# Gate weights' low parts by adding DMAs onto negated high parts, and an earlier place for a norm's parameters

## The chip, the core and the metric

The kernel runs on one core of a Trainium2 chip. A core has TensorE (PE, the matrix engine, with a weight-load queue PEld), VectorE (DVE), ScalarE (ACT), GpSimd (POOL) and SyncE (SP), each with a queue of instructions of its own that it works off in order, and 16 DMA engines that move data between the chip's main memory and the core's on-chip memory SBUF. Matmul results land in the banks of PSUM. The metric is the device time of one execution in microseconds.

## The reference

A decoder trunk of two layers over 256 rows of width 1024, all in float32. Each layer has four sub-layers, each followed by a norm over the residual sum:

```
x = LN(a*x + 0.5 * (silu(x Wgate) * (x Wup)) Wout)       first feed-forward
x = LN(a*x + mixer(x))                                     forgetting attention in layer 0, latent attention in layer 1
x = LN(a*x + 0.5 * (silu(x Wgate) * (x Wup)) Wout)       second feed-forward
x = LN(a*x + sigmoid(x Wg + bg) * (p[i] Wp))              gated sub-layer
```

LN subtracts the mean, divides by the deviation, multiplies by a gain vector g and adds a vector b. Layer 1's attention reads keys and values made from x at the end of layer 0 ("kv" below).

## The kernel before, in words

**Two parts for each operand.** A float32 matrix product is made of three products of rounded operands: the high part of a weight is the weight rounded to the matrix engine's format, its low part is the weight minus the high part; the same is done for x. The three products are high x high, high x low and low x high. So every weight is loaded raw from main memory, ACT copies it into a high part (line 246) and DVE subtracts that from the raw weight for the low part (line 247). A unit is half a load: 128x1024 elements of high and as many of low, in one slot (ten slots hl0 to hl9, and others on loan, named gb, qk, fs, ota, otb). Raw loads are groups of 1 MB or less in three buffers (raw), all issued by SP (lines 457 to 491); a buffer is free for the next group when both units of its last group have been split.

**Who orders the work.** The kernel runs its program once as a recorder, which yields the order in which units are used, and then for real. A planner (class Stream) follows estimated clocks of PE, ACT and DVE; after each triple of products it may put the next unit's split at that place of the ACT and DVE queues (`pump`, line 378), when the load should have come and ACT and DVE are not more than 1.6 us ahead of PE. A unit that is not split when it is needed is split there and then (`use`, line 390).

**The gated sub-layer** (`ple`, line 1052). The gate's weights Wg are eight units, key "pg", for both halves of the rows. The product x Wg is done for the first 128 rows (eight units, each three products into each of two banks), then for the last 128 rows with the same units. Before the last two units of the first half the transposes of the second half of x stand (`XT(1)`, line 1085); ACT and DVE make the two parts of the transposed x (xT, lines 623 and 627). After each half ACT takes the sigmoid (line 1075), DVE multiplies by the projected p (line 1076), adds to x and gathers statistics (lines 683, 684), POOL raises the variance to the power -1/2 (line 694), and DVE applies the norm in four instructions (line 702): two that subtract the mean and multiply by g, two that multiply by the root and add b, taken in turn for the two halves of the columns. g and b stand in one tile, gb, loaded by SP (line 668).

**What stands around it in layer 0.** Ahead of it the second feed-forward ends with its norm for each half of the rows, by the same lines 683 to 702. Behind it the queues go on with the weights of the shared keys (key "kd", 128x640 a unit) and those of layer 1's first feed-forward ("win", from in_ffn_in), whose products for the first rows come before the transposes of the last rows. In layer 1 the sub-layer is the end of the program: the second half of the rows goes by quarters of the columns, and SP stores x.

POOL in the kernel before issues no DMA; all of them are SP's.

Of the kernel before, what the change touches and what calls it, by code (L numbers as in the profile page):

```python
# [12 lines left out]
AF = mybir.ActivationFunctionType  # L13
ALU = mybir.AluOpType
# [14 lines left out]
SLACK_NS = 1600.0  # L29
# [100 lines left out]
class Recorder:  # L130
    def __init__(self):
        self.seq = []

    def use(self, key):
        self.seq.append(key)
        return Dummy()

    def pump(self, *a, **k):
        pass
# [5 lines left out]
class Stream:  # L145
# [74 lines left out]
    def split(self, half=False):  # L220
# [45 lines left out]
        self.pair(n)  # L266
        self.split_done(key, w)

    def aside(self, key):
        return self.side and key[0] == "ws" and key[-1] == 3  # L270

# [106 lines left out]
    def pump(self):  # L378

        if self.ready == len(self.order) or not self.free() or self.hold or self.order[self.ready] == self.stop:  # L380
            return
        arrival = self.arrives.get(group_of(self.order[self.ready]), 1e12)
        if arrival <= self.pe_t + 500 and max(self.act_t, self.dve_t) <= self.pe_t + SLACK_NS:
            key = self.order[self.ready]
            if self.sums_left(key):
                self.add(group_of(key))
            else:
                self.split()
# [19 lines left out]
def group_of(key):  # L408
    k = key[0]
    if k in ("win", "wiu", "fv", "kd", "dq"):  # L410
        return key[:-1] + (key[-1] // 2,)
    if k == "ws":
        return key[:-1]
    if k in ("wout", "fvb", "fvc", "fk", "fq", "fo", "pg", "pp", "mo", "qr"):
        return key[:-1] + (key[-1] // 2,)
    if k in ("kvk", "qn"):
        return ("kq", key[-1])
    return key
# [38 lines left out]
def make_loads(a):  # L457
    def loads(q, g, raw, fine, between):
        k, i = g[0], g[-1]
        if k in ("win", "wiu"):  # L460
            w = a[g[2]][0][g[1], g[3], i]
            if fine == 1:
                for k0 in range(4):
                    between.pop((i, k0), lambda: None)()
                    for h in range(2 if (i, k0) == (0, 0) else 1):
                        c = slice(512 * k0 + 256 * h, 512 * (k0 + 1) if i or k0 else 256 * (h + 1))
                        q.dma_start(raw[:, c], a["w00"][h] if (i, k0) == (0, 0) else a["w0"][4 * i + k0 - 1])
                return
            for k0 in range(0, 4, fine):
                c = slice(512 * k0, 512 * (k0 + fine))  # L470
                q.dma_start(raw[:, c], w[:, c])
        elif k in ("wout", "ws"):
            q.dma_start(raw, a[g[2]][1][g[1], i])
        elif k in ("fv", "fo", "mo", "fk", "fq"):
            q.dma_start(raw, a[k][i])
        elif k == "fvb":
            q.dma_start(raw, a[k])
        elif k in ("fvc", "qr"):
            w = a[f"{k}{i}"]
            q.dma_start(raw[:, 0 : w.shape[1]], w)  # L480
        elif k in ("pg", "pp"):
            q.dma_start(raw, a[k][g[1], i])
        elif k == "pb":
            q.dma_start(raw[0:1, 0:1024], a["ple_b_gate"][g[1] : g[1] + 1, :])
        elif k in ("kd", "dq", "kvv", "kq"):
            w = a[k][i]
            q.dma_start(raw[:, 0 : w.shape[1]], w)
        else:
            raise KeyError(g)

    return loads
# [13 lines left out]
class Trunk:  # L505
    def __init__(self, nc, pools, a, S, rec, fox_c=None):
        self.nc, self.a, self.S, self.fox_c = nc, a, S, fox_c
        self.sb, self.ps = pools
# [9 lines left out]
    def own(self, shape, dt, tag):  # L518

        self.S.check(tag)  # L520
        return self.tl(shape, dt, tag, 1)
# [8 lines left out]
    def home(self, homes):  # L530

        if self.rec:
            return None, Dummy()
        self.S.retire()
        tag = next(t for t in homes if t not in self.S.slot_of.values() and t not in self.taken)
        self.taken.add(tag)
# [6 lines left out]
    def use(self, key):  # L543
        w = self.S.use(key)
        if self.bg:
# [506 lines left out]
    def ple(self, li, last):  # L1052
        nc, S = self.nc, self.S
        y, st = {}, {}

        def bias(t, blocks):
            w = self.use(("pb", li))
            for c0, c1 in blocks:
                y[t, c0] = self.bank("y")
                self.mm(y[t, c0][:, 0 : c1 - c0], self.ones, w[:, 0, c0:c1], True, False)  # L1060

        def gate(t, k, blocks):
            w = self.use(("pg", li, k))
            for c0, c1 in blocks:
                self.mm3(
                    y[t, c0][:, 0 : c1 - c0], lambda i: self.xT[:, t, i, k, :],
                    lambda i: w[:, i, c0:c1], False, k == 7,
                )

        def post(t, c0, c1):  # L1070
            if t not in st:
                st[t] = [self.tl([128, 4, 6], F32, "st4", 2), self.tl([128, D], F32, "g4", 6), 0]
            s, sg, j = st[t]
            g = sg[:, c0:c1]
            nc.scalar.activation(g, y[t, c0][:, 0 : c1 - c0], AF.Sigmoid)
            nc.vector.tensor_tensor(g, g, self.pj[:, 2 * t + c0 // 512, c0 % 512 : c0 % 512 + c1 - c0], op=ALU.mult)  # L1076
            self.ln_stats(s[:, j, :], t, c0, c1 - c0, g, ALPHA)
            self.S.busy(act=c1 - c0, dve=c1 - c0)
            st[t][2] = j + 1

        full = ((0, 512), (512, 1024))
        bias(0, full)
        for k in range(8):
            if k == 6:
                self.XT(1)
            gate(0, k, full)
        for c0, c1 in full:
            post(0, c0, c1)
        self.ln_apply(0, st[0][0][:, 0:2, :], LN_EPS)
        quarters = tuple((c, c + 256) for c in range(0, 1024, 256))  # L1090
        if not last:
            bias(1, full)
            for k in range(8):
                if k == 6:
                    self.XT(0)
                gate(1, k, full)
            for c0, c1 in full:
                post(1, c0, c1)
            self.ln_apply(1, st[1][0][:, 0:2, :], LN_EPS)
            S.lend("ota")  # L1100
        else:
            self.store(0)
            for c0, c1 in quarters:
                bias(1, ((c0, c1),))
                for k in range(8):
                    gate(1, k, ((c0, c1),))
                post(1, c0, c1)
            self.ln_apply(1, st[1][0], LN_EPS, True)
            self.store(1, ENDS)
# [706 lines left out]
    def run(self):  # L1816
        S = self.S
        ple = lambda li: {6: [lambda: self.ple_load(li)]}
        self.ffn(0, "ffn1", 0, at={3: [self.load_x]}, cold=True, after=("ota", "otb", "qk"))
        self.fox(0)  # L1820
        self.ffn(0, "ffn2", 2, ple=True, at=ple(0), after=("otb", "qk", "fs"))
        self.load_gb(0, 3)
        self.kv_setup()
        self.ple(0, False)
        S.reclaim("fs")
        self.ffn(1, "ffn1", 0, kv=True, after=("otb", "qk"))
        self.mla(1)
        self.ffn(1, "ffn2", 2, ple=True, at=ple(1), after=("otb", "qk", "fs"))
        self.load_gb(1, 3)
        self.ple(1, True)  # L1830


@with_exitstack
def tile_trunk(ctx: ExitStack, tc: tile.TileContext, a):
    nc = tc.nc
    sb = ctx.enter_context(tc.tile_pool(name="sb", bufs=1))
    raw = ctx.enter_context(tc.tile_pool(name="raw", bufs=NRAW))
    ps = ctx.enter_context(tc.tile_pool(name="ps", bufs=1, space=bass.MemoryType.PSUM))
    dr = ctx.enter_context(tc.tile_pool(name="dr", bufs=1, space=bass.MemoryType.DRAM))
    ctx.enter_context(tc.manual_schedule())  # L1840
    a = dict(a)
    for n in ("ffn1", "ffn2"):
        a[n] = (a[n + "_in"], a[n + "_out"])
    r = Recorder()
    d = Dummy()
    Trunk(d, (d, d), d, r, True).run()
    S = Stream(nc, raw, sb, make_loads(a), r.seq)
    Trunk(nc, (sb, ps), a, S, False, dr.tile([16, 256], F32, name="fox_c")).run()


# [79 lines left out]
```

## Time and profile before

| | |
|---|---|
| median of 3 runs | 1053.96 us (1053.19 to 1055.26) |
| profiled execution | 1054.48 us |
| its span, first to last instruction | 1052.7 us |
| granted TensorE clock | 0.998 |
| gated sub-layer, layer 0 | PE from 484.6 to 510.2 us of the span |
| gated sub-layer, layer 1 | PE from 1019.9 to 1044.1 us |

Times in the profile are microseconds from the start of the span. In a timeline a row has the start, the duration, engine, line, operation, what it writes from what, shape and count; in brackets how long the engine stood idle before it and what ended that. A merged row with a count above one lasts from its first start to its last end. Instructions of DVE and ACT overlap a little: two copies of 1.04 us follow each other in 0.94. Matmul durations overlap too.

### The profile page before, as it was taken

What the parts mean: (1) busy time and instruction counts of PE and PEld (TensorE: products, weight loads), DVE (VectorE), ACT (ScalarE), POOL (GpSimd) and SP (SyncE); (2) the same over time, 40 slices, a digit from 0 to 9 for tenths busy, and PEclk for the clock granted to TensorE, in tenths of its full rate; (3) what the DMA queues carried; (4) which work ended last, traced back from release to release, by engine and by line L of the source; (5) the groups of instructions that cost most, each with busy time, mean ns of one, the idle gap of its engine ahead of it and who ended that gap; (6) DMA issues with size and microseconds to landing.
All of it is one profiled execution on the core that took longest, in us unless ns stands there. A gap on an engine that the chain in (4) does not pass through costs nothing.

```text
span 1052.7 us, 17554 instructions
## 1 busy us (share of the span) xinstructions
PE 1037.3 (99%) x7085; PEld 949.7 (90%) x7085; DVE 895.0 (85%) x1312; ACT 592.5 (56%) x901; POOL 59.9 (6%) x88
## 2 busy tenths in 40 slices
PE   9999999999999999999899999999999999999996
PEld 8999898999889999998799898988899889898986
DVE  5788976868898979978979899898887989899877
ACT  6565563667745554663465646546776564646541
POOL 0000000123300000000220000000000000000000
PEclk9999999999999999999999999999999999999999
DMA  7855586444736374673564555742444564554732
GB/s 280 307 186 188 194 287 242 161 144 159 257 126 240 120 249 144 219 301 140 190 234 157 201 195 168 277 154 105 151 155 170 184 213 156 184 213 174 279 121 81
DMA packets 37477, 202.74 MB, mean 193 GB/s; under 512 B 3970, under 2 KB 9874, under 8 KB 16532
## 3 DMA queue, kind: packets, MB, share of 16 engines
q1 hardware_dynamic: 37396, 201.63, 54.0%
q8 instruction: 55, 0.90, 0.3%
q14 instruction: 26, 0.21, 0.1%
HBM read 200.55 MB, written 1.06 MB: 192 GB/s over the span
## 4 chain that ended last, share of the span: by engine, by line
PE 68%; DVE 3%; ACT 1%; issue 1%; POOL 0%; DVEq 0%; ACTq 0%; POOLq 0%
PE h L610 37%; PE y L610 21%; PE tr L610 8%; PE tr L614 2%; DVE hl L247 1%; DVE x L702 0%; PE h L614 0%; DVE x L683 0%; DVE st L684 0%; DVE g L1076 0%; ACT hl L246 0%; POOL rs L694 0%; DVE tr L1715 0%; ACT qk L623 0%; ACT P L1340 0%
## 5 line engine op out<-in xcount | busy, mean ns | idle before, releaser
L610 PE MATMUL h<-xT,hl 128*128 128x256 f32 x3144 | 366.9, 278 | 0.2 <-DVE hl L323 0.2
L610 PEld LDWEIGHTS h<-xT,hl 128*128 128x128 f32 x3144 | 362.8, 189 | 2.0 <-ACT xT L623 0.6
L247 DVE TENSOR_TENSOR hl<-raw,hl 128x1024 fp32r<-128x1024 f32 (+4 forms) x273 | 317.3, 1191 | 38.8 <-ACT hl L246 37.6
L246 ACT ACTIVATE hl<-raw 128x1024 fp32r<-128x1024 f32 (+4 forms) x273 | 270.0, 1027 | 72.0 <-DVE raw L302 41.0
L610 PE MATMUL y<-hl,g 128*128 128x512 f32 x336 | 78.6, 391 | 0.0
L610 PEld LDWEIGHTS y<-hl,g 128*128 128x128 f32 x336 | 62.6, 188 | 12.6
L610 PE MATMUL h<-hl,xT 128*128 128x512 f32 (+2 forms) x312 | 68.0, 371 | 0.0
L610 PEld LDWEIGHTS h<-hl,xT 128*128 128x128 f32 x312 | 54.9, 188 | 9.8
L610 PE MATMUL y<-hl,otb 128*128 128x512 f32 x219 | 58.0, 399 | 0.0
L610 PE MATMUL y<-hl,xT 128*128 128x512 f32 (+3 forms) x282 | 52.7, 334 | 0.0
L623 ACT ACTIVATE xT<-tr 128x512 fp32r<-128x512 f32 x28 | 16.3, 597 | 61.7 <-PE tr L614 61.6
L258 DVE TENSOR_TENSOR hl<-raw,hl 128x1024 fp32r<-128x1024 f32 (+2 forms) x42 | 49.7, 1188 | 1.3 <-ACT hl L254 1.2
L254 ACT ACTIVATE hl<-raw 128x1024 fp32r<-128x1024 f32 (+2 forms) x42 | 43.0, 1028 | 9.7 <-DVE raw L302 9.2
L610 PEld LDWEIGHTS y<-hl,xT 128*128 128x128 f32 x282 | 44.1, 188 | 4.6 <-ACT xT L623 0.4
L610 PEld LDWEIGHTS y<-hl,otb 128*128 128x128 f32 x219 | 39.8, 188 | 8.3 <-DVE otb L627 0.3
L610 PE MATMUL y<-hl,ota 128*128 128x512 f32 x177 | 46.7, 398 | 0.1
L694 POOL TENSOR_TENSOR rs<-ve,mhalf 128x1 f32<-128x1 f32 x16 | 15.1, 944 | 522.2 <-DVE ve L693 522.2
L610 PE MATMUL tr<-xT,hl 128*128 128x256 f32 x360 | 42.8, 278 | 0.0
L610 PEld LDWEIGHTS tr<-xT,hl 128*128 128x128 f32 x360 | 42.1, 188 | 0.3
L610 PEld LDWEIGHTS y<-hl,ota 128*128 128x128 f32 x177 | 32.8, 189 | 7.7 <-DVE hl L247 0.6
L820 ACT ACTIVATE P<-h 128x512 f32<-128x512 f32 x33 | 19.7, 596 | 33.2 <-PE h L610 32.8
L294 DVE TENSOR_TENSOR ts<-raw 128x1024 f32<-128x1024 f32 x29 | 35.4, 1222 | 0.6
(324 smaller groups left out, 1638.5 us busy)
## 6 DMA issues: line engine op xcount, KB each, us to landing
raw<-in_ffn_in_dram SPq DMA_DIRECT2D x85, 1024.0 KB, 4.9
raw<-in_ffn_out_dram SPq DMA_DIRECT2D x44, 1024.0 KB, 5.0
raw<-in_pg_dram SPq DMA_DIRECT2D x8, 1024.0 KB, 4.8
raw<-in_mo_dram SPq DMA_DIRECT2D x8, 1024.0 KB, 4.8
raw<-in_kq_dram SPq DMA_DIRECT2D x8, 640.0 KB, 4.2
gb<-in_ln_g_dram SPq DMA_DIRECT2D x8, 512.0 KB, 6.2
gb<-in_ln_b_dram SPq DMA_DIRECT2D x8, 512.0 KB, 7.6
raw<-in_fk_dram SPq DMA_DIRECT2D x4, 1024.0 KB, 5.0
```

The source lines that it names most:

```text
L246: nc.scalar.activation(hi, src, AF.Copy)
L247: nc.vector.tensor_tensor(lo, src, hi.bitcast(F32), op=ALU.subtract)
L254: nc.scalar.activation(hi, src, AF.Copy)
L258: nc.vector.tensor_tensor(lo, src, hi.bitcast(F32), op=ALU.subtract)
L294: tt(s[:, 0:1024].rearrange("p (a b) -> p a b", b=512), r[:, 0:512][:, None, :].to_broadcast([128, 2, 512]), r[:, 512:1536].rearrange("p ( ...
L610: self.nc.tensor.matmul(out, lhsT, rhs, start=start, stop=stop)
L614: self.nc.tensor.transpose(out, in_, self.ident)
L623: self.nc.scalar.activation(hi, src, AF.Copy)
L694: nc.gpsimd.tensor_tensor(rs, ve, self.mhalf, op=ALU.pow)
L820: nc.scalar.activation(gt, ps, AF.Silu)
```

## The change

For the units "pg" alone the low part is made without DVE. ACT writes the high part and, with a second copy of scale -1, its negative into the place of the low part. Then POOL issues a DMA that adds the raw weight, read once more from main memory, onto that place; what stands there afterwards is the weight minus its high part. The planner asks ACT's clock alone for such a unit, and marks it as done when the DMA is issued; PE's products wait for the DMA itself. Besides, the parameters of the sub-layer's norm (gb) are asked for ahead of its first half's seventh unit and no more before the sub-layer.

```diff
+    def summed_by_dma(self, key):
+        return key[0] == "pg"
+
+    def split_by_dma(self):
...
+        w = self.place(key, slot)
+        self.nc.scalar.activation(w[:, 0, :n], src, AF.Copy)
+        self.nc.scalar.activation(w[:, 1, :n], src, AF.Copy, scale=-1.0)
+        u = key[-1] % 2
+        self.nc.gpsimd.dma_start(
+            w[:, 1, :n], self.a[key[0]][key[1], key[-1] // 2][:, 1024 * u : 1024 * u + 1024], accum_op=ALU.add)
+        self.busy(act=n)
+        self.busy(act=n)
+        self.split_done(key, w)
...
+        if self.summed_by_dma(self.order[self.ready]):
+            if arrival <= self.pe_t + 500 and self.act_t <= self.pe_t + SLACK_NS:
+                self.split_by_dma()
+            return
         if arrival <= self.pe_t + 500 and max(self.act_t, self.dve_t) <= self.pe_t + SLACK_NS:
...
             if k == 6:
+                self.load_gb(li, 3)
                 self.XT(1)
...
-        self.load_gb(0, 3)
         self.kv_setup()
...
-        self.load_gb(1, 3)
         self.ple(1, True)
```

The planner's clocks move other instructions with it. In the rows of the new kernel the line numbers are higher by 20 to 25: 280 and 281 are the two copies, 283 is the adding DMA, and 651, 718, 726 and 1100 are what was 627, 694, 702 and 1076. The first place is DVE's queue in layer 0, from the last row of the first rows' gated norm (x_69) to the product of the last rows (x_70 and its g). Before:

```order
L702 SCALAR_TENSOR_TENSOR x_69<-x_69,rs,gb 128x512
L247 TENSOR_TENSOR hl_5387<-raw,hl_5387 128x640
L247 TENSOR_TENSOR hl_5395<-raw,hl_5395 128x1024
L627 TENSOR_TENSOR xT<-tr_5398,xT 128x512
L627 TENSOR_TENSOR xT<-tr_5405,xT 128x512
L247 TENSOR_TENSOR hl_5418<-raw,hl_5418 128x1024
L247 TENSOR_TENSOR hl_5429<-raw,hl_5429 128x1024
L1076 TENSOR_TENSOR g_5433<-g_5433,ota 128x512
```

And now:

```order
L726 SCALAR_TENSOR_TENSOR x_69<-x_69,rs,gb 128x512
L247 TENSOR_TENSOR hl_5391<-raw,hl_5391 128x1024
L247 TENSOR_TENSOR hl_5400<-raw,hl_5400 128x1024
L247 TENSOR_TENSOR hl_5411<-raw,hl_5411 128x1024
L651 TENSOR_TENSOR xT<-tr_5414,xT 128x512
L651 TENSOR_TENSOR xT<-tr_5421,xT 128x512
L247 TENSOR_TENSOR otb<-raw,otb 128x1024
L247 TENSOR_TENSOR qk<-raw,qk 128x1024
L1100 TENSOR_TENSOR g_5449<-g_5449,ota 128x512
```

Five units of the feed-forward's weights are split there instead of three, otb and qk among them; before, otb came behind the norm that this product begins. The last unit of "kd" (128x640) has moved to the front of the first rows' norm.

The second place is POOL's queue in layer 0, from the zeroing for the gate's bias row to the roots (rs) of the norms. Before, the one row behind the zeroing holds all four roots:

```order
L250 MEMSET hl_5077 128x1024
L694 TENSOR_TENSOR rs<-ve,mhalf 128x1 x4
L1444 TENSOR_TENSOR rs<-ve,mhalf 128x1
L1459 TENSOR_SCALAR PT<-PT,rs 128x256
L1460 TENSOR_TENSOR PT<-PT,nrm 128x256
```

Now:

```order
L250 MEMSET hl_5077 128x1024
L283 DMA hl_5091<-in_pg_dram 128x1024
L283 DMA hl_5098<-in_pg_dram 128x1024
L283 DMA otb<-in_pg_dram 128x1024
L283 DMA qk<-in_pg_dram 128x1024
L283 DMA fs<-in_pg_dram 128x1024
L718 TENSOR_TENSOR rs<-ve,mhalf 128x1
L283 DMA hl_5175<-in_pg_dram 128x1024
L283 DMA hl_5199<-in_pg_dram 128x1024
L283 DMA hl_5206<-in_pg_dram 128x1024
L718 TENSOR_TENSOR rs<-ve,mhalf 128x1 x3
```

Five adding DMAs stand ahead of the first root and three between it and the second. In layer 1 four stand ahead of the first and four behind.

The third place is SP's queue in layer 0, behind the gate's loads. Before:

```order
L482 DMA raw<-in_pg_dram 128x2048 x4
L487 DMA raw<-in_kd_dram 128x1280 x2
L541 DMA gb<-in_ln_g_dram 128x1024
L541 DMA gb<-in_ln_b_dram 128x1024
L541 DMA nrm<-in_kv_norm_dram 128x256
L541 DMA rope<-in_rope_dram 128x128 x2
L471 DMA raw<-in_ffn_in_dram 128x2048 x10
```

Now:

```order
L506 DMA raw<-in_pg_dram 128x2048 x4
L511 DMA raw<-in_kd_dram 128x1280 x2
L495 DMA raw<-in_ffn_in_dram 128x2048
L565 DMA nrm<-in_kv_norm_dram 128x256
L565 DMA rope<-in_rope_dram 128x128 x2
L495 DMA raw<-in_ffn_in_dram 128x2048
L565 DMA gb<-in_ln_g_dram 128x1024
L565 DMA gb<-in_ln_b_dram 128x1024
L495 DMA raw<-in_ffn_in_dram 128x2048 x8
```

The norm's parameters have moved behind two loads of feed-forward weights. On ACT the sixteen copies of the eight units stand in one piece ahead of the copies of xT, broken only by one row of the projected p.

More of the change, by code (lines that the diff above doesn't have):

```diff
@@ L267, in split @@
         self.split_done(key, w)
+    def summed_by_dma(self, key):
+        return key[0] == "pg"
+    def split_by_dma(self):
+        self.later()
+        key = self.order[self.ready]
+        src, _, n = unit_of(key, self.raw[group_of(key)])
+        slot = self.slots.pop(0)
+        self.slot_of[key] = slot
+        w = self.place(key, slot)
[7 more added lines that the diff above has]
+        self.split_done(key, w)
     def aside(self, key):
@@ L1847, in tile_trunk @@
     S = Stream(nc, raw, sb, make_loads(a), r.seq)
+    S.a = a
     Trunk(nc, (sb, ps), a, S, False, dr.tile([16, 256], F32, name="fox_c")).run()
```

## The prediction

> **What bounds the kernel now.** I read the page first (shares), then the waits of TensorE (PE), then the timelines of PE, VectorE (DVE) and ScalarE (ACT) in the two stages the change touches, and the chain that ended last.
>
> ```profile
> span 1052.7 us, 17554 instructions
> PE 1037.3 (99%) x7085; PEld 949.7 (90%) x7085; DVE 895.0 (85%) x1312; ACT 592.5 (56%) x901; POOL 59.9 (6%) x88
> ```
>
> PE is busy for 99% of the span and its work is untouched, so this change can only win where PE stands still. The waits of PE (engine, line, what it waited for: total us, times, longest) are few:
>
> ```profile
> PE h L610 <- DVE otb L247: 3.0, 1, 3.0
> ...
> PE tr L614 <- DVE x L702: 0.7, 1, 0.7
> ```
>
> Both lie around the gated sub-layer of layer 0. In PE's timeline (start, us, what, count, idle before it), the step at 506.93 is late by 0.71, the one at 521.20 by 2.99:
>
> ```profile
> 505.62 0.60 PE L614 MATMUL tr<-ident,x 128*128 128x128 f32 x4
> 506.93 0.63 PE L614 MATMUL tr<-ident,x 128*128 128x128 f32 x4 [0.71 <-DVE x L702]
> ...
> 517.82 0.40 PE L610 MATMUL h<-otb,xT 128*128 128x512 f32 x1
> 521.20 1.43 PE L610 MATMUL h<-otb,xT 128*128 128x512 f32 x5 [2.99 <-DVE otb L247]
> ...
> 525.22 1.03 PE L614 MATMUL tr<-ident,x 128*128 128x128 f32 x8
> ...
> 528.41 0.63 PE L610 MATMUL h<-ota,xT 128*128 128x512 f32 x2
> ```
>
> DVE is what is late: it makes the low part of that otb (a unit of the next feed-forward's weights) at 519.93, right behind the norm of the second half of the rows:
>
> ```profile
> 519.20 0.75 DVE L702 SCALAR_TENSOR_TENSOR x<-x,rs,gb 128x512 f32<-128x512 f32 x1
> ...
> 519.93 1.22 DVE L247 TENSOR_TENSOR otb<-raw,otb 128x1024 fp32r<-128x1024 f32 x1
> ```
>
> So the ceiling of the gain is 2.99 + 0.71 = 3.70 us. The gated sub-layer of layer 1 has no PE wait at all; it ends the program, and there the chain is PE without a break until its last matmul:
>
> ```profile
> 1029.60 14.52 PE y L610 x112
> 1044.12 0.02 issue
> 1044.15 0.39 ACT g L1075
> ```
>
> What comes earlier in front of that changes nothing: layer 1 can only lose.
>
> **What the change removes, and what moves up.** Per layer it takes eight low parts from DVE. Rows of DVE in layer 0:
>
> ```profile
> 473.80 1.22 DVE L247 TENSOR_TENSOR fs<-raw,fs 128x1024 fp32r<-128x1024 f32 x1 [1.03 <-ACT fs L246]
> ...
> 480.76 0.75 DVE L702 SCALAR_TENSOR_TENSOR x<-x,rs,gb 128x512 f32<-128x512 f32 x1
> ...
> 484.55 1.22 DVE L247 TENSOR_TENSOR hl<-raw,hl 128x1024 fp32r<-128x1024 f32 x1 [0.26 <-ACT hl L246]
> ...
> 486.29 0.68 DVE L683 SCALAR_TENSOR_TENSOR x<-x,y 128x512 f32<-128x512 f32 x1
> ...
> 492.66 2.35 DVE L247 TENSOR_TENSOR hl<-raw,hl 128x1024 fp32r<-128x1024 f32 x2
> ...
> 498.85 0.69 DVE L1076 TENSOR_TENSOR g<-g,ota 128x512 f32<-128x512 f32 x1 [0.43 <-ACT g L1075]
> ...
> 506.03 0.75 DVE L702 SCALAR_TENSOR_TENSOR x<-x,rs,gb 128x512 f32<-128x512 f32 x1
> ...
> 512.04 0.68 DVE L1076 TENSOR_TENSOR g<-g,ota 128x512 f32<-128x512 f32 x1
> ```
>
> Five of the eight lie before 475.1 us, and DVE stands idle among them (1.03 in the first row); the norm that follows takes sums that PE finishes about then. They are worth nothing. Without the one at 484.55 the norm at 486.29 starts about 1.0 us sooner. Those at 492.66 make room for the low parts of the next weights (line 247, 128x640). The gate's product at 498.85 waits for ACT, whose rows say why:
>
> ```profile
> 469.15 1.04 ACT L246 ACTIVATE otb<-raw 128x1024 fp32r<-128x1024 f32 x1
> 470.09 1.04 ACT L246 ACTIVATE qk<-raw 128x1024 fp32r<-128x1024 f32 x1
> 472.70 1.06 ACT L246 ACTIVATE fs<-raw 128x1024 fp32r<-128x1024 f32 x1 [1.57 <-DMA raw<-in_pg_dram]
> 482.97 0.60 ACT L623 ACTIVATE xT<-tr 128x512 fp32r<-128x512 f32 x1 [9.20 <-PE tr L614]
> ...
> 494.92 1.99 ACT L246 ACTIVATE hl<-raw 128x640 fp32r<-128x640 f32 x3
> 496.93 1.28 ACT L1075 ACT_TABLE_LOAD   x1
> ```
>
> Three copies stand in front of the table load; in the new order one does, the other three copies of that weight having moved ahead of the transposes. Two copies less are 2 x 0.66 = 1.3 us: the product starts at about 497.6, the norm behind it ends at 506.70 - 1.25 = 505.45, and PE's wait of 0.71 is gone.
>
> Then comes the piece that matters. By the new order DVE makes three low parts, two of xT, then those of otb and qk, and only then the second norm. With steps of 1.13 (492.66: 2.35 for two) and 0.62 for xT: 505.45 + 3 x 1.13 + 2 x 0.62 + 2 x 1.13 = 512.35. So otb is ready near 511.2, almost 6 us before PE wants it (517.82 - 0.71 = 517.1), and the 2.99 us are gone. What is late next: the second norm starts at 512.35 instead of 512.04 and ends near 520.3; PE, 3.70 us ahead, wants the transposes of its result at 525.22 - 3.70 = 521.5. Slack 1.2. Behind it DVE still owes three low parts and one product (0.4), to 524.2; PE wants the last one (the place of ota above) at 528.41 - 3.70 = 524.7. Slack 0.5. Both hold, thinly: I keep 3.0 to 3.7 for this term, 3.5 as its value.
>
> **What it adds on ACT.** A second copy per unit: sixteen copies in a row instead of eight, at the step of 470.09 - 469.15 = 0.94, from 466.77 (the first one's start in the chain of rows above, two steps and one 0.5 us copy ahead of 469.15). 466.77 + 16 x 0.94 + 0.5 = 482.3; the copies of xT behind them can start at 482.97, when PE's transposes are done. Cover 0.7 us, and 0.8 more before PE misses xT: nothing.
>
> **What it adds on POOL.** Eight DMA issues per layer, in front of the reciprocal roots of the norms (line 694): five ahead of the first in layer 0, four in layer 1.
>
> ```profile
> 478.36 0.93 POOL L694 TENSOR_TENSOR rs<-ve,mhalf 128x1 f32<-128x1 f32 x1 [26.14 <-DVE ve L693]
> ...
> 521.65 2.03 POOL L1459 TENSOR_SCALAR PT<-PT,rs 128x256 f32<-128x256 f32 x1
> ...
> 470.53 0.33 SPq L482 DMA_DIRECT2D raw<-in_pg_dram  x1
> ```
>
> No DMA of POOL is in this trace. Bounds for one issue: 0.33 us (SyncE's own, last row) and 2.03 (POOL's dearest row of this stretch). From the first unit's copies, done at 468.6, five issues of 2.03 end at 478.8: the root is 0.4 late, and the rows it feeds (the norm ends at 481.5) are wanted by PE's transposes some 0.6 before the copy at 482.97, the first of them taking only the half of x that is done 1.4 us sooner. So the root can be 2 us late for nothing, and an issue cost 2.3. I take 1 us an issue and a cost of 0.
>
> **What it adds on the DMA engines.** Sixteen transfers that add 512 KB each. Plain loads in the DMA issues (KB, median us to landing):
>
> ```profile
> raw<-in_pg_dram SPq DMA_DIRECT2D x8, 1024.0 KB, 4.8
> ...
> raw<-in_kvv_dram SPq DMA_DIRECT2D x4, 512.0 KB, 3.5
> ```
>
> So 512 KB more cost 1.3 us, and 2.2 are fixed. An adding transfer costs the engines at least the 1.3 of its source; at most I count it as a load of 1024 KB, source and old sum, 2.6. Time there is for them in layer 0: the first can move at about 469.7, the last unit is wanted near 495.5 and has to be through some 1.5 us earlier:
>
> ```profile
> 494.10 3.00 PE L610 MATMUL y<-hl,xT 128*128 128x512 f32 x12
> ```
>
> (two units of 1.37). That is 24.3 us. In them the engines also carry the loads that SyncE issues: about 2 us left of the third pg load, one more pg load and one of the next feed-forward (2.6 each), two of 640 KB (1.6 each), 10.4 together, since the raw buffers now come free after ACT alone. 13.9 are left, 1.74 per adding transfer. Below that nothing waits; each 0.1 above costs 0.8 us. In layer 1 the stretch is as long and only the pg loads compete, 4.6 us: (24.3 - 4.6)/8 = 2.46 are free there. I take a price under 1.74, nearer the 512 KB row: only 512 KB come from main memory and 512 KB are written. Cost 0, and 0 to 8 us kept for the range (2.6: 6.9 in layer 0 and 1.0 in layer 1).
>
> [...]
>
> **The norm's parameters.** Before, SyncE stands at gb until the norm ends, and the feed-forward's load waits behind it:
>
> ```profile
> 492.77 0.33 SPq L541 DMA_DIRECT2D gb<-in_ln_g_dram  x1
> ...
> 495.10 2.94 SPq L471 DMA_DIRECT2D raw<-in_ffn_in_dram  x2
> ```
>
> Now one such load goes before it with nothing to wait for but its buffer, a second before gb waits for DVE's low parts behind the norm, at about 493.2; gb follows at 493.5, behind that load's 2.6 us and with the 3.6 that it takes to land alone:
>
> ```profile
> DMA to landing us min/median/max: 3.6/3.6/3.6
> ```
>
> Landed near 499.7, wanted four rows of 0.75 before the norm's end and a little sooner, at 502.1: cost 0, slack 2.4. In layer 1 nothing moves past it.
>
> **The sum.** Profiled execution: 1054.48 (span 1052.7 and 1.8 around it). -3.5 (PE's two waits) + 0 + 0 + 0 + 0 = 1051.0. The median of the runs is 0.5 below the profiled one, so 1053.96 - 3.5 = 1050.5. A difference of 0.2%, 2.1 us, is about what a measurement of this kernel can tell from no change.
>
> **Rivals.**
> 1. *The adding transfers read twice.* At 2.6 each the last units land late and PE waits inside the first gate: -3.5 + 6.9 + 1.0 = +4.4, 1058.4. It decides against the change from 1.74 + 3.5/8 = 2.2 on, and it is slower by over 0.2% from about 2.45. For it: an add needs the old value, and between 470 and 475 the DMA engines are 96% busy already (the last two figures of this row: share, GB/s). Against it: the copies pace the transfers, 1.9 us apart, and half of what is read is on the chip. [...] Chance 0.26.
>
> ```profile
> 470.00:475.00 5.00, 5.00 (x24) 4.14 (x23) 3.97 (x4) 2.20 (x3) 0.00 (x0) 1.00 0.96 380
> ```
>
> 2. *Transfers late by about what is won* (1.9 to 2.45 each), or DVE's thin slack of 0.5 gone, so that the wait moves from 518 to 524: 1051.9 to 1056, about 1053.5. For it: the slacks above. Against it: the window of prices is narrow. Chance 0.21.
> 3. *POOL's queue holds the root.* At 3 us an issue five end at 483.6, the root is 5.3 us late, 3.3 of them in PE's sight: 1053.8; at 4 us 8.3, and about 4 in layer 1, where four stand ahead of it: 1062.8. For it: none of these issues is in the trace. Against it: no POOL row here lasts that long. Chance 0.07, counted as slower.
>
> **How the numbers follow.** Forecast (everything hidden, 1049.8 to 1051.9): 0.46. Rivals 0.26, 0.21 and 0.07. Faster 0.46; same 0.21; slower 0.26 + 0.07 = 0.33. The range goes from 1049.7 (all 3.70, and 0.5 for the scatter of the runs, 1053.19 to 1055.26) up to 1059.5, which takes in a price of 2.6 and leaves out what is above 2.75, about 0.1.
>
> **What would show it.** Right: no PE wait on otb near 518 and none on x near 506, DVE's line 247 for otb before the second norm; the new DMAs' landing under 4 us alone, the eighth unit landed before PE's 494 and 1029. Wrong: PE waiting for a DMA inside the first gate matmuls (485 to 496, 1020 to 1031), or line 694 starting later than 480 in layer 0, or PE waiting on line 702 or 247 at 521 to 525.

## The result, and the profile after

The changed kernel takes 1059.62 us (median of 5 runs, 1059.16 to 1062.42) against 1053.96: ratio 1.0056, 95% interval 1.004 to 1.0072. It is slower by 5.7 us; the forecast was 3.5 us faster. The first rival of the prediction (1058.4, adding transfers that count twice) came within 1.2 us.

The page's first lines, as of the kernel before. VectorE's (DVE's) busy time has fallen by 20 us as it should (16 low parts). PE's idle time has grown by 2.4 us (15.4 to 17.8), and its busy time by 3.1, in part because matmuls ran at half clock (0.50 granted from 495 to 498 us, last section):

```profile
span 1058.2 us, 17598 instructions
...
PE 1040.4 (98%) x7085; PEld 949.2 (90%) x7085; DVE 875.1 (83%) x1296; ACT 607.9 (57%) x917; POOL 69.9 (7%) x104
```

The waits of PE (total us, times, longest). Those on otb's low part and, at 506, on x are gone; the x of this list is an earlier one, and in the gate PE now waits for DMAs:

```profile
PE y L634 <- DMA fs<-in_pg_dram: 2.2, 1, 2.2
PE tr L638 <- DVE x L726: 1.6, 1, 1.6
...
PE y L634 <- DMA hl<-in_pg_dram: 1.0, 1, 1.0
```

PE's timeline in layer 0 gives the places. The first row is the last piece of the feed-forward, which I use as the zero of this stage; the bias row of the second half of the rows (ones) closes the first half of the gate:

```profile
466.82 15.12 PE L634 MATMUL y<-hl,g 128*128 128x512 f32 x66
483.51 0.63 PE L638 MATMUL tr<-ident,x 128*128 128x128 f32 x4 [1.57 <-DVE x L726]
...
494.99 2.50 PE L634 MATMUL y<-fs,xT 128*128 128x512 f32 x5 [2.24 <-DMA fs<-in_pg_dram]
...
503.26 1.43 PE L634 MATMUL y<-hl,xT 128*128 128x512 f32 x5 [1.01 <-DMA hl<-in_pg_dram]
504.53 0.63 PE L634 MATMUL y<-hl,ones 128*128 128x512 f32 x2
...
528.62 1.03 PE L638 MATMUL tr<-ident,x 128*128 128x128 f32 x8
```

The same three places in the kernel before:

```profile
467.37 15.12 PE L610 MATMUL y<-hl,g 128*128 128x512 f32 x66
...
496.93 0.63 PE L610 MATMUL y<-hl,ones 128*128 128x512 f32 x2
...
525.22 1.03 PE L614 MATMUL tr<-ident,x 128*128 128x128 f32 x8
```

From the zero to the bias row it was 29.56 us and is 37.71: 8.15 lost in the first half of the gate. From the bias row to the transposes of the next feed-forward it was 28.29 and is 24.09: 4.20 won, the two waits that were to go and 0.5 more. So the gain came in full, and the loss in front of it is twice as large. Layer 1 loses 0.9 by the same count (1002.62 to 1032.19 before, 1006.89 to 1037.36 now). Another 0.9 lies between the two gates, 0.63 of it a wait of PE for VectorE at 575.24; no experiment placed it.

Two things could be behind the 8.15. First, the DMA queues in the stretch from 455 to 535 us (packets, MB, share of the 16 engines' time):

```profile
q1 hardware_dynamic: 2865, 15.16, 52.2%
q0 software_dynamic: 1152, 4.19, 26.7%
```

q0 carries the eight adding DMAs: 26.7% of 80 us are 21.4, or 2.67 us of all 16 engines for each. Second, POOL's queue:

```profile
476.04 0.88 POOL L283 DMA_DIRECT2D qk<-in_pg_dram  x1 [2.42 <-DVE st L708]
481.13 0.86 POOL L283 DMA_DIRECT2D fs<-in_pg_dram  x1 [4.20 <-issue]
481.70 0.88 POOL L718 TENSOR_TENSOR rs<-ve,mhalf 128x1 f32<-128x1 f32 x1
...
491.29 0.83 POOL L283 DMA_DIRECT2D hl<-in_pg_dram  x1 [5.10 <-issue]
495.25 0.87 POOL L283 DMA_DIRECT2D hl<-in_pg_dram  x1 [3.13 <-issue]
```

An issue itself takes the 0.83 to 1.04 us that I assumed. But POOL stands 3 to 5 us ahead of some of them for "issue", that is for nothing that the profile shows, while the copies they need are long made. The root (line 718) stands behind the fifth and starts at 481.70 instead of 478.36, 3.9 us later when both are counted from their zero rows; that is PE's wait of 1.57 at 483.51.

### The profile page after: what moved, and what is told of

It reads as the page before. It is cut to its first block, busy times and chain, and to the rows that moved or that the text cites. A ratio compares the mean times of both kernels' runs of the same rounds, so it can differ in the third digit from the quotient of the medians.

```text
span 1058.2 us, 17598 instructions
## 1 busy us (share of the span) xinstructions
PE 1040.4 (98%) x7085; PEld 949.2 (90%) x7085; DVE 875.1 (83%) x1296; ACT 607.9 (57%) x917; POOL 69.9 (7%) x104
## 3 DMA queue, kind: packets, MB, share of 16 engines
HBM read 208.94 MB, written 1.06 MB: 198 GB/s over the span
## 4 chain that ended last, share of the span: by engine, by line
PE 62%; issue 5%; DVE 4%; DMA 1%; POOL 1%; ACT 1%; POOLq 0%; DVEq 0%; ACTq 0%
PE h L634 35%; PE y L634 18%; PE tr L634 7%; DMA hl<-in_pg_dram 1%; PE tr L638 1%; DVE hl L247 1%; POOL hl L283 0%; PE h L638 0%; DVE ts L314 0%; DVE hl L258 0%; DVE ts L320 0%; DVE x L726 0%; DVE st L708 0%; DVE tr L1740 0%; POOL rs L718 0%
## 5 line engine op out<-in xcount | busy, mean ns | idle before, releaser
L247 DVE TENSOR_TENSOR hl<-raw,hl 128x1024 fp32r<-128x1024 f32 (+5 forms) x261 | 302.1, 1188 | 33.8 <-ACT hl L246 32.7
L246 ACT ACTIVATE hl<-raw 128x1024 fp32r<-128x1024 f32 (+5 forms) x261 | 257.7, 1026 | 68.2 <-DVE raw L322 36.7
L647 ACT ACTIVATE xT<-tr 128x512 fp32r<-128x512 f32 x28 | 16.0, 595 | 52.2 <-PE tr L638 52.2
L634 PE MATMUL tr<-xT,hl 128*128 128x256 f32 x336 | 39.6, 277 | 0.1
L634 PEld LDWEIGHTS tr<-xT,hl 128*128 128x128 f32 x336 | 38.8, 188 | 0.5 <-DVE hl L247 0.3
L726 DVE SCALAR_TENSOR_TENSOR x<-x,rs,gb 128x512 f32<-128x512 f32 (+1 forms) x33 | 24.1, 735 | 16.8 <-POOL rs L718 15.8
```

The costliest lines, as they stand in the source:

```text
L246: nc.scalar.activation(hi, src, AF.Copy)
L247: nc.vector.tensor_tensor(lo, src, hi.bitcast(F32), op=ALU.subtract)
L634: self.nc.tensor.matmul(out, lhsT, rhs, start=start, stop=stop)
L647: self.nc.scalar.activation(hi, src, AF.Copy)
L726: nc.vector.scalar_tensor_tensor(xs, xs, rs if i else mv[:, 0:1], self.gb[:, i, c0:c1], op0=ALU.mult if i else ALU.subtract, op1=ALU.add i ...
```

## The experiments

Two theories, both for the 8.15 us. **Price**: an adding DMA of 512 KB takes some 2.6 us of all DMA engines (q0 above) where a plain one takes 1.4 (q1: 15.16 MB in 52.2% of 80 us), and the stage has not that much of them to give. **Ring**: what the program sets aside for POOL's DMAs (`dynamic_dma_scratch_size=1024`; the expectations call it the descriptor memory) takes three adding DMAs; the fourth issue stands until the oldest has landed, and the root and all later issues stand behind it. The name is the theory's: the runs show what the issues do at 1,024 and at 2,048, not what lies there.

Each ratio is to the kernel before on the same chip, with its 95% interval. "Engine time" is what the gate's transfers (q0, and q10 where there is one) take of all 16 engines between 455 and 535 us, the share times 80. "Late" is the way from the zero row to the bias row, less the 29.56 of before; "net" is the same up to the transposes of the next feed-forward, less 57.85.

| run | ratio | engine time | late | net |
|---|---|---|---|---|
| the change | 1.0056 (1.004 to 1.0072) | 21.4 | 8.15 | +3.95 |
| e1 larger ring | 1.008 (1.0067 to 1.0093) | 21.3 | 9.11 | +4.96 |
| e2 its control | 1.0057 (1.0045 to 1.007) | 21.3 | 8.17 | +3.97 |
| e3 plain copies | 0.9961 (0.9949 to 0.9974) | 11.7 | 0.00 | -4.02 |
| e4 gb moved alone | 0.9998 (0.9988 to 1.0007) | 0 | 0.01 | +1.57 |
| e5 extra on POOL's queue | 1.032 (1.0302 to 1.0337) | 26.0 | 22.95 | +18.94 |
| e6 last three units | 0.9955 (0.994 to 0.9969) | 9.0 | 0.01 | -4.02 |
| e7 three by POOL | 1.0021 (1.0012 to 1.0031) | 0 | 6.61 | +2.41 |
| e8 two by POOL | 0.9965 (0.9951 to 0.9978) | 0 | 1.30 | -2.70 |
| e9 half adds | 0.9964 (0.9952 to 0.9976) | 11.8 | 0.07 | -3.95 |
| e10 plain and traffic | 1.002 (1.0011 to 1.003) | 19.0 | 5.66 | +1.50 |
| e11 first five units | 0.9991 (0.9982 to 1.0) | 13.5 | 3.11 | -0.92 |
| e12 layer 0 alone | 1.0035 (1.0023 to 1.0047) | 21.4 | 8.52 | +4.34 |

"Late" and "net" are each read from one trace, and hold what PE's clock cost in that trace (last section); the ratios are over all runs.

**e1 and e2: the ring.**

```diff
-nc = ...(..., dynamic_dma_scratch_size=1024)
+nc = ...(..., dynamic_dma_scratch_size=2048)
...
-self.kvn = self.tl([128, QR], F32, "nrm", 1)[:, 0:256]
+self.kvn = self.tl([128, 256], F32, "nrm", 1)
-qn = self.tl([128, QR], F32, "nrm", 1)
+qn = self.tl([128, 1536], F32, "ts", 1)[:, 0:QR]
-raw = self.tl([128, 128], F32, "p1", 1)
+raw = self.tl([128, 1536], F32, "ts", 1)[:, 0:128]
```

e2 has the last three edits and 1024. Expected of e1:

> The changed kernel with twice the descriptor memory of POOL's DMA queue (2,048 bytes of each partition instead of 1,024); to make room, two small buffers of layer 1's attention (the query norm's parameters, one head's raw block) share another's place. Theory ring (POOL's queue takes only three adding DMAs at a time, and its fourth issue and the norm's root stand behind the oldest one's landing): the eight issues of layer 0 follow each other at the pace of ACT's copies, the root of 481.7 us comes at about 478.5, PE's waits of 2.2 and 1.6 us go, and the time is 1050.5 to 1052.5. Theory price (an adding DMA takes some 2.6 us of all 16 DMA engines where a plain one takes 1.4): the root comes on time, but the last units still land late, PE loses some 5 to 6 us before the second half instead of 8.3, and the time is 1056 to 1058.

And of e2:

> The changed kernel with the two small buffers placed as in the run with the larger descriptor memory, but with the memory as it was (1,024): the control for it. Both theories: 1059.6, within 0.8 us of the changed kernel.

POOL's timeline in e1:

```profile
478.08 0.85 POOL L283 DMA_DIRECT2D fs<-in_pg_dram  x1 [1.04 <-ACT fs L281]
479.32 0.94 POOL L718 TENSOR_TENSOR rs<-ve,mhalf 128x1 f32<-128x1 f32 x1 [0.39 <-DVE ve L717]
```

At 2,048 no issue stands any more, and the root waits for DVE alone (0.39 us): the size of 1,024 was what held POOL. Yet e1 is no faster than e2; by the ratios it is slower (1.008 against 1.0057). PE's waits say why: the transposes are on time, and what was waited there is waited in the gate.

```profile
PE y L634 <- DMA fs<-in_pg_dram: 2.3, 1, 2.3
PE y L634 <- DMA qk<-in_pg_dram: 1.7, 1, 1.7
PE y L634 <- DMA hl<-in_pg_dram: 1.3, 3, 0.7
```

The low part of the last unit sets the end of the first half in both runs, in e1 and then in e2:

```profile
505.74 1.42 PE L634 MATMUL y<-hl,xT 128*128 128x512 f32 x5 [0.44 <-DMA hl<-in_pg_dram]
```

```profile
504.84 1.43 PE L634 MATMUL y<-hl,xT 128*128 128x512 f32 x5 [0.98 <-DMA hl<-in_pg_dram]
```

Counted from the zero rows (468.33 and 468.38) it comes at 37.41 us in e1 and at 36.46 in e2. So the ring is real and its removal won nothing here: the same 21.3 us of transfers set the end, whoever queues. Why the last transfer lands 0.95 later in e1, although it is issued sooner, is open. Theory ring falls as the cause. Theory price put e1 at 1056 to 1058, that is a gain of some 2 us from the root; there was none. e2 is the change again, at its ratio (1.0057), so the moved buffers cost nothing.

**e3: plain copies.** The same DMA without its add.

```diff
-[...][:, 1024 * u : 1024 * u + 1024], accum_op=ALU.add)
+[...][:, 1024 * u : 1024 * u + 1024])
```

> The changed kernel with the adding DMAs made plain copies (the same 512 KB each, issued by POOL at the same places, but without the add: the low part is then the raw weight, so the product is another). Theory price: the software queue's share of the DMA engines' time falls from 4.0% to about 2.1% (1.4 us a transfer), the last units land 4 us and more earlier, and the time is 1050 to 1052.5. Theory ring alone (the price is not what counts): the share falls all the same, but POOL still stands at its fourth and later issues until an older one has landed, some 5 us behind its issue each, and the root is still late by 1 to 2 us: 1053 to 1056.

The product is another one, since this kernel leaves out the add. The queue of e3 in the stretch from 455 to 535:

```profile
q0 software_dynamic: 1152, 4.19, 14.6%
```

The same packets and bytes cost 1.46 us a transfer instead of 2.67, nothing is late (466.04 to 495.60 from the zero to the bias row), and the ratio is 0.9961: the forecast's gain, with the add alone taken away. POOL no longer stands either, so e3 by itself does not part price from ring; with e1 it does.

**e9: half an add.** Adds over 512 of 1024 columns.

```diff
-w[:, 1, :n], [...][:, 1024 * u : 1024 * u + 1024], accum_op=ALU.add)
+w[:, 1, 0:512], [...][:, 1024 * u : 1024 * u + 512], accum_op=ALU.add)
```

> The changed kernel with each adding DMA cut to its first 512 columns (256 KB in rows of 2 KB; the second half of a low part stays the negated high part, so the product is another). Theory price, by bytes: the software queue's share falls from 4.0% to 2.0 to 2.3%, about that of the whole plain copies (2.3%), and the ratio is theirs, 0.996 to 0.998. Theory latency (an add lands late whatever its size, or costs by the row): the share stays over 3% and the ratio over 1.001.

Its queue in the same stretch:

```profile
q0 software_dynamic: 1152, 2.10, 14.8%
```

256 KB of adding cost 1.48 us, as much as 512 KB of plain copy, and the ratio (0.9964) is the plain one's. As many adding DMAs as in the change do no harm when the engine time fits. The price goes nearly by bytes and not by rows: the packets are as many as before, and the price falls from 2.67 to 1.48. The ring still holds POOL's queue here:

```profile
478.79 0.86 POOL L283 DMA_DIRECT2D fs<-in_pg_dram  x1 [3.50 <-DVE x L726]
```

This fifth issue starts when the second transfer has landed (478.6), and the root behind it comes at 479.36, 12.87 us from the zero row where it was 10.99 before. These 1.9 us are inside the 2 that the prediction found free. So e9 keeps three adding DMAs at a time, with a shorter standing and about half the price, and loses nothing; e1 has the price without the standing and is 9.11 late.

**e10: plain copies and other traffic.** Behind e3's copy, on ACT's own queue:

```diff
+self.nc.scalar.dma_start(
+    self.spare[8 * key[1] + key[2]], [...][:, 1024 * u : 1024 * u + 672])
...
+S.spare = [dr.tile([128, 672], F32, name=f"spare{i}") for i in range(16)]
```

> Plain copies as in the run without the add, and beside each, on ACT's own DMA queue, a transfer of 336 KB of the same weight from main memory to a place of its own in main memory, on which nothing waits: some 1.2 us more of all 16 engines a unit, by the run in which such a copy stood on POOL's queue, and no add anywhere. Theory price (it is the DMA engines' time that runs out, not the add): the units land late again, PE waits for DMAs in the gate, ratio 1.002 to 1.009. Theory latency of the add: nothing waits for the extra transfers, ratio 0.996 to 0.998.

Its queues between 455 and 535 (q10 is the extra one), and PE's waits:

```profile
q0 software_dynamic: 1152, 4.19, 14.1%
q10 hardware_dynamic: 1152, 2.75, 9.6%
```

```profile
PE y L636 <- DMA qk<-in_pg_dram: 1.7, 1, 1.7
PE y L636 <- DMA fs<-in_pg_dram: 1.6, 1, 1.6
```

With no add anywhere, and on POOL no standing, the gate waits for its DMAs again and is 5.66 us late: 1.002. It is engine time that runs out (DMA share 0.97 to 1.14 from 488 to 502 us), not something that only an add does.

**e5: a failed form of e10.** The second copy stood on POOL's queue and wrote one and the same place each time; the size of 2,048 and the moved buffers are e1's.

```diff
+self.nc.gpsimd.dma_start(self.spare, [...][:, 1024 * u : 1024 * u + 1024])
```

> Plain copies as in the run without the add, the larger descriptor memory, and behind each plain copy a second transfer on POOL's queue of the same 512 KB from main memory to an unused place in main memory: no add anywhere, but the DMA engines get about as much more work as the add had brought. Theory price (engine time, whatever it is spent on): the software queue's share rises to 4% and more, raw weights and low parts land late again, and the ratio to the kernel before is 1.005 to 1.010, like that of the adding DMAs with the larger memory (1.008). Theory latency (an adding DMA lands late by itself, the others do not suffer): the low parts land as in the plain run, and the ratio is 0.996 to 0.998.

POOL's waits in e5:

```profile
POOL spare L285 <- DMA spare<-in_pg_dram: 59.3, 14, 7.4
```

Each write of that place had to wait for the one before it, 59.3 us in all, and the norms' roots stood behind on POOL. It tells nothing between the theories, only what a held POOL queue can cost: PE waited 30.4 us for norms.

**e6: the last three units of layer 0 alone.**

```diff
-return key[0] == "pg"
+return key[:2] == ("pg", 0) and key[2] >= 5
```

> The changed kernel with adding DMAs for the last three gate units of layer 0 alone (the only low parts that stood in VectorE's way); the other 13 are VectorE's again. Theory ring: three fit, POOL never stands, root on time, and the ratio is 0.9965 (3.7 us gained). Theory price: 1.2 us of more engine time each, 3.6 in all, and the last units' low parts land some 6 us behind their copies, so PE waits 1.5 to 3 us in units 5 to 7 and keeps 1 to 2 us of the gain: 0.998 to 0.999.

The queue between 455 and 535, and POOL:

```profile
q0 software_dynamic: 432, 1.57, 11.2%
```

```profile
478.14 0.93 POOL L718 TENSOR_TENSOR rs<-ve,mhalf 128x1 f32<-128x1 f32 x1 [26.14 <-DVE ve L717]
479.03 2.98 POOL L283 DMA_DIRECT2D hl<-in_pg_dram  x3
```

0.9955, faster than both kernels: all of the gain and nothing late. My expectation by price (PE waits 1.5 to 3 us in these units) missed. With five units' traffic gone the raw weights come sooner (ACT's copy of the seventh unit starts 9.8 us from the zero row, against 12.9 in the change), the three issues follow the root at 479, and what PE needs from 491.7 on has landed by then: it waits for no DMA in this stage. Theory ring had 0.9965 for it, but e6 does not part the two: three transfers fit into the ring, and 9.0 us fit into the 13.9 of the prediction. A transfer costs 3.0 us here, a little more than the 2.67 of the change.

**e11: the first five units alone.**

```diff
-return key[0] == "pg"
+return key[:2] == ("pg", 0) and key[2] < 5
```

> Adding DMAs for the first five units of layer 0 alone, the ones whose low parts VectorE had time for; the last three and layer 1 are VectorE's, as before. No gain is left (the waits of 3.0 and 0.7 us come from the last three). Theory price: 5 x 1.2 us of engine time too much for the raw weights and the units behind, ratio 1.000 to 1.005. Theory ring: the fourth and fifth issue hold the root by 2 us, ratio 1.001 to 1.003; the two are told apart by PE's waits (on DMAs, or on the norm).

POOL's timeline and PE's wait in e11:

```profile
480.63 0.88 POOL L283 DMA_DIRECT2D fs<-in_pg_dram  x1 [5.26 <-issue]
481.20 0.89 POOL L718 TENSOR_TENSOR rs<-ve,mhalf 128x1 f32<-128x1 f32 x1
```

```profile
PE tr L638 <- DVE x L726: 1.8, 1, 1.8
```

Here the ring is alone: it holds the root, PE waits for the norm and for no DMA, and 3.11 us are lost before the bias row. But the total is no loss (0.9991), and both expectations missed that: PE's later waits of 3.0 and 0.7 are gone, though DVE still makes the last three low parts. For the 3.0 the rows show why:

```profile
511.90 1.21 DVE L247 TENSOR_TENSOR otb<-raw,otb 128x1024 fp32r<-128x1024 f32 x1
```

```profile
518.90 1.55 PE L634 MATMUL h<-otb,xT 128*128 128x512 f32 x6
```

DVE's queue has the change's order here too, with otb ahead of the second norm, so this low part is made some 6 us before PE takes it; it would have been in time for a PE that is not 3.11 us late. The wait of 0.7 is gone by a hair and with the help of PE's own lateness: x is done at 507.37 and the transposes start at 507.46. What the order alone would win, with no low part moved, was not tried.

**e7 and e8: POOL subtracts.** The low parts of units 5 to 7 (e7) or 6 and 7 (e8) of layer 0.

```diff
-self.nc.scalar.activation(w[:, 1, :n], src, AF.Copy, scale=-1.0)
-self.nc.gpsimd.dma_start(...)
+self.nc.gpsimd.tensor_tensor(w[:, 1, :n], src, w[:, 0, :n].bitcast(F32), op=ALU.subtract)
...
```

> No adding DMA: the low parts of the last three gate units of layer 0 are subtracted by POOL instead of VectorE, the other 13 by VectorE as before. Both theories of the loss: no more traffic, no ring, so what remains is POOL's own duration. The 128x256 row (0.74 us) puts a 128x1024 one at up to 3.0 us, three in a row from 484.6 to 493.6, with the second root of 489.2 behind the second or third of them: 2 to 4 us late against 1.2 us of slack. Ratio 0.997 to 1.000.

> As the run with POOL's subtraction for three units, but for the last two alone (units 6 and 7 of layer 0): 2.35 us taken from VectorE right where it is late, and POOL done by about 492. The root of 489.2 may stand behind the first or the second, 1 to 3 us. Ratio 0.997 to 0.999.

POOL's timeline in e8, then in e7:

```profile
488.80 2.41 POOL L281 TENSOR_TENSOR hl<-raw,hl 128x1024 fp32r<-128x1024 f32 x1 [6.75 <-ACT hl L280]
...
493.25 2.39 POOL L281 TENSOR_TENSOR hl<-raw,hl 128x1024 fp32r<-128x1024 f32 x1
```

```profile
482.78 7.93 POOL L281 TENSOR_TENSOR hl<-raw,hl 128x1024 fp32r<-128x1024 f32 x3
```

A subtraction takes 2.4 us alone. Two give 0.9965 (expected 0.997 to 0.999), three give 1.0021 (expected up to 1.000). In e7 PE waits 4.2 us for x at 491.41, but not because a root stood behind POOL, as I had expected: the roots followed DVE at once. DVE's own rows of e7 show the cause:

```profile
482.84 2.89 DVE L722 SCALAR_TENSOR_TENSOR x<-x,rs,gb 128x512 f32<-128x512 f32 x1 [0.45 <-POOL rs L714]
485.65 2.87 DVE L722 SCALAR_TENSOR_TENSOR x<-x,mv,gb 128x512 f32<-128x512 f32 x1
488.55 2.71 DVE L722 SCALAR_TENSOR_TENSOR x<-x,rs,gb 128x512 f32<-128x512 f32 x1
```

Three passes over x last 2.7 to 2.9 us instead of 0.75, each about as long as one of POOL's three subtractions (7.93 us together). In e8 one does (2.88 at 493.32), beside POOL's second. In e7 the norm stood beside the subtractions. Not every pass is longer beside POOL: in e8 DVE's four passes beside the first subtraction (from 489.06 to 491.8, lines 703 and 704) kept their 0.7 us. The longer ones read x and gb, these four x and PE's y, or x alone; whether that is the reason no run shows. In e7 the clock is at half late in PE's wait of 4.2 and behind it (0.56 from 489 to 491, 0.50 to 496), which is some 2.2 us of the 6.61.

**e12 and e4.** Layer 0 alone (`key[:2] == ("pg", 0)`), and the kernel before with only the gb load moved.

> The changed kernel with adding DMAs in layer 0 alone. Layer 1 was read to lose 0.9 us of its own: ratio 1.0045 to 1.005 where the changed kernel has 1.0056. If layer 1 loses more than the trace showed: under 1.004.

> The kernel before with only the other half of the change, the norm parameters' load moved to the seventh unit of the gate's first half; no adding DMA. Both theories: the move is free, 1054.0, within 0.8 us of the kernel before; none of the 5.7 us comes from it. If it does cost, SP's queue would show the gb loads ahead of a weight that PE then waits for, and the time would be above 1055.

e12 gives 1.0035 where 1.0045 to 1.005 was expected. Layer 1 thus costs 2 us by the medians of the ratios, 0.9 by the trace, and the intervals of e12 and the change overlap: no finer than that. e4 shows nothing (0.9998), as expected; the net of +1.57 in its trace is clock (last section).

## Why the prediction was wrong, step by step

**The gain was right.** 3.5 was forecast for the two waits of layer 0. e3 and e6 have 4.02 at the transposes of the next feed-forward, and the change itself has 4.20 from the bias row on. In e11 the last three low parts stay on VectorE and the 3.0 is gone all the same, so that part goes with the new order of VectorE's queue, which the prediction called the piece that matters; how much the low parts taken from VectorE add to it is open.

**The step that failed is the price of an adding transfer**: "I take a price under 1.74, nearer the 512 KB row: only 512 KB come from main memory and 512 KB are written. Cost 0". It is 2.67. The argument counted what crosses to main memory, and that count was right. The page has

```profile
HBM read 208.94 MB, written 1.06 MB: 198 GB/s over the span
```

and e3's plain copies read the same 208.94 MB. But the engines' time goes by something else. Two full stretches of layer 1, the change with adds alone, and e10 with plain copies and extra traffic (the last two figures are the DMA share and GB/s):

```profile
1019.00:1029.00 10.00, 10.00 (x47) 7.67 (x46) 6.16 (x11) 4.87 (x6) 2.74 (x4) 1.00 1.06 211
```

```profile
1013.00:1026.00 13.00, 12.94 (x60) 10.09 (x59) 8.53 (x16) 7.24 (x9) 3.07 (x5) 1.00 1.08 402
```

Full engines move 211 GB/s of adds and 402 of copies, a ratio of 0.52. So an add onto SBUF ran at about half the rate of a copy; why, no run here shows. The first rival had this price, as an estimate from the plain loads (a load of 1024 KB, source and old sum). I gave it 0.26 because no row showed an adding transfer. The plain rows were the nearest, and the one of 1024 KB fitted (2.6 against 2.67), not the one of 512 KB that I took.

**The budget was right.** The prediction found 13.9 us of engine time free for the gate's transfers in layer 0, with every microsecond above it lost. The table bears it out: 9.0, 11.7 and 11.8 are not late, 13.5 waits for no DMA, 19.0 is 5.66 late (5.1 by the budget), 21.4 is 8.15 (7.5). That the sizes agree so well is partly luck: 2.07 of the 8.15 are lost behind the held root before the gate's first weight matmul, and e1, with the root on time, is 9.11 late for 21.3 (7.4).

**POOL's issue: duration right, cover wrong.** One issue takes 0.9 us as assumed ("I take 1 us an issue and a cost of 0"). That the queue can stand for 3 to 5 us at an issue was not in the sum; the root came 3.9 us late. The third rival had this consequence, from an issue of 3 us that does not exist. e1 shows that its removal gains nothing while the price stands, e11 that it costs 3.1 us in its stage where the price does not count, e9 that a root 1.9 us late costs nothing.

**The rest.** ACT's second copies cost nothing: in e3, with all sixteen of them, the first transposes and the bias row come as before. The moved gb load is free (e4). Layer 1 could only lose, and lost about 1 us, as the first rival put it.

## What to carry to other kernels

Before work is moved from an engine to an adding DMA, count the DMA engines' free time in that very stage, and price the add at nearly twice a copy of its size: 2.67 against 1.46 us for 512 KB here. Move only what stands in the way: with three of the sixteen low parts moved the kernel is 0.45% faster (0.994 to 0.9969 of before) instead of 0.56% slower. And look at what the move does to the order of the other queues: part of the gain came with the order, which may be had for less (not tried). Look, too, at what else lives on the queue that issues: an issue that stood held everything behind it here, the root by 3.9 us.

## What the runs showed of the hardware that was not expected

**POOL's queue took three adding DMAs at a time** with `dynamic_dma_scratch_size=1024`. In the change the fourth to the eighth issue start 0.2 to 0.3 us after the first to the fifth transfer have landed (by their times to landing at 475.7, 480.9, 485.1, 491.0 and 494.9; the issues at 476.04, 481.13, 485.30, 491.29 and 495.25). Half the bytes in as many rows stand in the same way (e9). With 2,048 no issue stands, with six under way at most (e1). In e3, with 1,024, plain copies did not stand: the eighth was issued at 481.77 with four others under way by their landing times, so the three of the change are no limit for copies. A plain issue also took less of POOL: 0.54 us by the median against 0.87.

**Behind waits of 2 us PE's clock was at half, and the length of a wait alone does not decide.** Windows of the change, granted clock third from the right:

```profile
495.00:496.00 1.00, 1.00 (x2) 0.81 (x3) 0.00 (x0) 0.00 (x0) 0.75 (x2) 0.50 1.10 219
...
498.00:499.00 1.00, 1.00 (x4) 0.87 (x5) 0.96 (x3) 0.00 (x0) 0.00 (x0) 0.88 1.05 219
```

After the wait of 2.24 us the clock is at half for a good 3 us, some 1.7 us of work that no row of the waits lists. It did not set the end here: PE stands 1.01 us more for the last unit's low part at 503.26, and with a full clock it would have stood there the longer. In e1 the clock is at half from about 497 to 504, among them:

```profile
502.00:503.00 1.00, 1.00 (x8) 1.00 (x6) 0.00 (x0) 0.50 (x1) 0.00 (x0) 0.50 0.99 271
```

There too PE stands for the last unit behind it (0.44 at 505.74), so as far as these rows show the clock is not why e1 is behind e2. In e2 it is at half for about 3 us (0.50 from 487 to 489), behind PE's wait of 1.92 for the norm. In e10 waits of 1.73 and 1.61 left the clock at 1.00, and so did the one of 2.99 in the kernel before:

```profile
522.00:523.00 1.00, 1.00 (x6) 0.83 (x5) 1.00 (x2) 0.34 (x2) 1.00 (x1) 1.00 0.82 147
```

The same wait in e4, where this stage is otherwise as before, did not:

```profile
522.00 1.70 PE L610 MATMUL h<-otb,xT 128*128 128x512 f32 x5 [2.99 <-DVE otb L247]
```

```profile
523.00:524.00 1.00, 1.00 (x4) 0.73 (x3) 1.00 (x2) 0.27 (x1) 1.00 (x1) 0.50 0.56 115
```

e4's clock is at half until about 526. No later wait of the stage hides that, and it is the whole of the +1.57 in the table. So the length of the wait alone does not decide. The clock was at half behind 1.92 and 2.24 us, at 1.00 behind 1.73 and 1.61, and behind 2.99 once the one and once the other; what else decides, no run here shows.
